# A hybrid decoder layer on one core: block tiles for h, its sums on two engines, and another order of the block products

## The chip, the core and the metric

The kernel runs on one core of a Trainium2 chip. The core has TensorE (PE: matmuls into PSUM), VectorE (DVE), ScalarE (ACT) and GpSimd (POOL) for element-wise work, and SyncE (SP), which here issues every DMA from one queue. Each engine runs its own instructions in order and waits for semaphores of the others. The metric is the time of one execution in microseconds; the kernel before was run three times, and one further execution was profiled. All data are float32. A matmul operand is split into two parts of the type fp32r, hi = round(x) and lo = x - hi, and a product is three matmuls: hi·hi, hi·lo and lo·hi.

## The reference, cut to what matters

```python
h    = rms_norm(x, g_pre)                       # (1024, 1024)
proj = h @ w_in                                 # q,k,v,z_a | u,v_s,z_s | z_m,xBC,dt | 3 x 1024 gate logits
y_att = sliding_window_attention(q, k, v, sinks, rel_bias) * silu(z_a)
y_sg  = u * (tril(w_s) @ LN(v_s) + b_s) * silu(z_s)     # by chunk of 128 rows and group of 128 channels
y_ssm = ssd_mixer(z_m, xBC, dt, ...)            # conv, chunked scan, gated group norm
merged = sum over i of sigmoid(gate_i) * (y_i @ w_br_i)
out    = x + rms_norm(merged @ w_out, g_post)
```

## The kernel before

The sequence has 1024 rows and the model 1024 channels. `hT` holds h transposed, channels on the partitions, as one tile of hi and one of lo parts, each 128 x 8 x 1024; every projection reads it. The work goes through these stages:

1. h is made and transposed (`norm`, `flip`), and the first columns are projected.
2. For each of four groups of the state-space mixer: convolution units, then a scan over eight chunks (`Mix`). `local` makes, for a chunk, the product of B and C and a transposed copy of B in one PSUM tile (pool `ps_tr`, two tiles); DVE masks the product into `gtm` (L549), and ACT copies B into `btok` (L551). `sums` needs a tile of the same pool (L602). Between the scan's small products a stream of projection units (`st`) is run by `st.fill`.
3. Attention, with q, z_a and v_s units in the same stream. A v_s unit takes two weight tiles; `load_w` loads a weight, ACT casts whi (L87) and DVE makes wlo (L88). For each 128 rows the result is copied by ACT (L636) and its row statistics are made by DVE (L637, `bst`), both from PSUM.
4. The sums of h. The u, z_s and half of the gate columns are projected by a scheme of seven products in place of eight for a 2 x 2 split of h (rows by channels) and of w. It needs four sums of the blocks of h: s1, s2, s3, s4. For each of four slices kt POOL adds hi and lo of the four blocks (r, L839), and forms the sums (L842 to L845); ACT and DVE split them into hi and lo (L828, L829). s3 overwrites block (1, 0) of h, once the last v_s product has read it. Beside it run the last v_s tiles.
5. The pair stage. `PairStream` runs units of seven products, 12 matmuls each. A unit loads two weight tiles (`raw`), POOL forms four sums of them (`ts`, L207), ACT and DVE split each operand four products ahead (L224, L225). Every product goes into the pool `ps_mm`, three tiles. What follows a product is in the code: s1, u2, u3, s5 are temporaries in a ring of six (`tp`), and four blocks of the result leave as z (blocks 11 and 21) and u (12 and 22). Eight `zu` units come first, with their silu, the mixing product `sg_mix` and its loads `sg_load` between products by an estimate of their time; six `gate_pair` units follow, whose blocks go through a tanh to DRAM.
6. The branch products. `load_y` fetches one of 32 tiles y from DRAM into `yraw` (two buffers), scales the first 16 by `rsb` on POOL (L962), and splits them on ACT and DVE (L964, L965; y4 and y5 of the first eight on POOL). Twelve slots hold them; three (NPY) can be filled before the space of h is given back. `br_unit` is a projection of eight y's; the first unit takes its operands in the pieces 3, 1, 1, 1, 1, 1. After four units of a set the y's of the next set are loaded, and then the stream is emptied.
7. The output product, its norm and the sum with x.

TensorE's order is that of the code. The order on the other engines is set by a scheduler when the program is built; each keeps to it when it runs.

## Time and profile before

| | |
|---|---|
| runs, median (lowest to highest) | 1917.54 us (1916.57 to 1923.05) |
| profiled execution | 1924.31 us |
| its span | 1922.6 us, mean granted TensorE clock 0.977 of full speed |
| busy, share of the span | PE 95%, DVE 57%, ACT 38%, POOL 30% |

The profile records one execution. A row of a wait names the instruction that waited, the one that released it, and the idle time. A row of a stretch gives the busy time of each engine in it and the TensorE clock that was granted, 1.00 being 2.4 GHz and 0.50 being 1.2 GHz. An engine's idle time costs something only where TensorE waits for it in the end.

### The profile page before, as it was taken

The page shows a single profiled execution, that of the slowest core. Times are in us where ns is not written, and L with a number is a line of the kernel's source. Part 1 is how long each engine was busy: PE and PEld are TensorE (multiplying, and loading weights), DVE is VectorE, ACT ScalarE, POOL GpSimd, SP SyncE. Part 2 cuts the span into 40 slices and gives each one's busy share as a digit, 9 for nine tenths or more (in the row PEclk, how much of TensorE's full clock was granted, in tenths as well). Part 3 has the DMA queues.
Part 4 walks back from the last instruction along what each step waited for, and adds up shares of the span by engine and source line. Part 5 has one row for each costly group of instructions (what it writes and reads, how often), then busy time and mean ns, then how long its engine had stood idle before and what let it go on. Part 6 is the DMA issues. An engine that isn't in the chain of part 4 may idle for free. (4 is left out here: it accounts for less than half of the span.)

```text
span 1922.6 us, 24786 instructions
## 1 busy us (share of the span) xinstructions
PE 1827.9 (95%) x9481; PEld 1540.4 (80%) x9481; DVE 1101.1 (57%) x1546; ACT 724.5 (38%) x1551; POOL 570.9 (30%) x570
## 2 busy tenths in 40 slices
PE   6999999999999999999999779999996999999998
PEld 6888788778877877888888777777885878888898
DVE  5446656675665657466666348887743343535424
ACT  5244454355345434455555222222432120202221
POOL 1001420240132024156666766555724110000000
PEclk9999999999999999999999989999997999999999
DMA  6211431342234134211111122333435453533213
GB/s 218 72 58 55 121 126 44 99 141 62 64 118 121 44 107 127 102 44 56 44 56 56 64 72 73 117 103 116 148 115 203 143 166 97 175 109 111 88 34 143
DMA packets 100663, 192.86 MB, mean 100 GB/s; under 512 B 9376, under 2 KB 55744, under 8 KB 100416
## 3 DMA queue, kind: packets, MB, share of 16 engines
q1 hardware_dynamic: 100544, 191.28, 30.8%
q8 instruction: 74, 1.21, 0.3%
q14 instruction: 45, 0.37, 0.1%
HBM read 152.83 MB, written 38.42 MB: 99 GB/s over the span
## 5 line engine op out<-in xcount | busy, mean ns | idle before, releaser
L105 PE MATMUL ps_mm<-hT,whi 128*128 128x512 f32 x1104 | 436.6, 395 | 0.8 <-DVE z L317 0.8
L107 PE MATMUL ps_mm<-hT,wlo 128*128 128x512 f32 x1104 | 430.2, 390 | 0.0
L106 PE MATMUL ps_mm<-hT,whi 128*128 128x512 f32 x1104 | 430.1, 390 | 0.0
L87 ACT CAST whi<-raw 128x1024 fp32r<-128x1024 f32 (+1 forms) x119 | 124.1, 1043 | 338.1 <-PE ps_mm L106 317.0
L105 PEld LDWEIGHTS ps_mm<-hT,whi 128*128 128x128 f32 x1104 | 207.4, 188 | 44.3 <-issue 2.5
L107 PEld LDWEIGHTS ps_mm<-hT,wlo 128*128 128x128 f32 x1104 | 207.3, 188 | 44.0
L106 PEld LDWEIGHTS ps_mm<-hT,whi 128*128 128x128 f32 x1104 | 207.7, 188 | 40.9
L88 DVE TENSOR_TENSOR wlo<-raw,whi 128x1024 fp32r<-128x1024 f32 (+1 forms) x117 | 152.2, 1302 | 117.7 <-ACT whi L87 117.6
L105 PE MATMUL ps_mm<-y,whi 128*128 128x512 f32 x512 | 202.8, 396 | 12.3 <-ACT y L964 12.3
L106 PE MATMUL ps_mm<-y,whi 128*128 128x512 f32 x512 | 203.2, 397 | 7.1 <-DVE y L965 3.8
L107 PE MATMUL ps_mm<-y,wlo 128*128 128x512 f32 x512 | 202.3, 395 | 0.0
L558 POOL TENSOR_TENSOR y<-xg,dsk 128x512 f32<-128x512 f32 x32 | 39.5, 1245 | 389.8 <-issue 225.5
L499 DVE SCALAR_TENSOR_TENSOR acc<-xr,wcv,acc 128x512 f32<-128x512 f32 x144 | 111.4, 773 | 40.5 <-ACT acc L497 37.1
L105 PEld LDWEIGHTS ps_mm<-y,whi 128*128 128x128 f32 x512 | 98.0, 191 | 34.5 <-ACT y L964 14.1
L106 PEld LDWEIGHTS ps_mm<-y,whi 128*128 128x128 f32 x512 | 97.9, 191 | 30.4 <-DVE y L965 5.7
L107 PEld LDWEIGHTS ps_mm<-y,wlo 128*128 128x128 f32 x512 | 98.0, 191 | 20.4
L78 POOL TENSOR_TENSOR rso<-rso,mhalf_row 128x1 f32<-128x1 f32 x8 | 4.4, 552 | 353.6 <-DVE rso L77 353.6
L996 DVE SCALAR_TENSOR_TENSOR tm<-gld,ps_mm 128x512 f32<-128x512 f32 x48 | 33.0, 687 | 131.5 <-PE ps_mm L107 131.4
L130 PE MATMUL ps_mm<-whi,hT 128*128 128x256 f32 (+1 forms) x256 | 83.0, 324 | 25.7 <-DVE bst L637 11.8
L247 PE MATMUL ps_mm<-hT,whi 128*128 128x512 f32 x224 | 89.8, 401 | 10.3 <-DVE us L259 6.0
L534 ACT ACTIVATE seg<-seg,acs 128x128 f32<-128x128 f32 x256 | 80.9, 392 | 28.2 <-DMA seg<-acs_dr 28.1
L249 PE MATMUL ps_mm<-hT,wlo 128*128 128x512 f32 x224 | 88.6, 396 | 0.0
(223 smaller groups left out, 3728.6 us busy)
## 6 DMA issues: line engine op xcount, KB each, us to landing
seg<-acs_dr SPq DMA_DIRECT2D x32, 512.0 KB, 4.7
yraw<-y_dr SPq DMA_DIRECT2D x32, 512.0 KB, 4.5
raw<-in_w_br_dram SPq DMA_DIRECT2D x32, 512.0 KB, 4.2
gld<-gate_dr SPq DMA_DIRECT2D x32, 512.0 KB, 3.4
raw<-in_w_xbc_dram SPq DMA_DIRECT2D x24, 512.0 KB, 3.6
raw<-in_w_zm_dram SPq DMA_DIRECT2D x16, 512.0 KB, 3.5
y_dr<-y SPq DMA_DIRECT2D x32, 256.0 KB, 2.2
raw<-in_w_zu_dram SPq DMA_DIRECT2D x16, 512.0 KB, 3.7
```

The costliest lines, as they stand in the source:

```text
L87: A.copy(hi, raw)
L88: eng.tensor_tensor(lo, raw, hi.bitcast(F32), op=ALU.subtract)
L105: T.matmul(ps, lhsT=whi[:, ks], rhs=rhs(0, kt, half), start=kt == 0, stop=False)
L106: T.matmul(ps, lhsT=whi[:, ks], rhs=rhs(1, kt, half), start=False, stop=False)
L107: T.matmul(ps, lhsT=wlo[:, ks], rhs=rhs(0, kt, half), start=False, stop=kt == KT - 1)
L130: T.matmul(o, lhsT=lhs(0, kt, tt), rhs=whi[:, ks], start=kt == 0, stop=False)
L247: T.matmul(o, lhsT=hi[:, ks], rhs=h0, start=kt == 0, stop=False)
L249: T.matmul(o, lhsT=lo[:, ks], rhs=h0, start=False, stop=kt == 3)
L499: V.scalar_tensor_tensor(acc, xr[:, k + f0:k + f0 + 512], wcv[:, ti, k:k + 1], acc, op0=ALU.mult, op1=ALU.add)
L534: A.activation(seg[:, j, :], seg[:, j, :], AF.Relu, scale=-1.0, bias=acs[:, c, g * 8 + j:g * 8 + j + 1])
L558: G.tensor_tensor(d["y"], xg[g][:, :, cs], col(dsk, g), op=ALU.mult)
L996: V.scalar_tensor_tensor(tm, gt[0][:, fs], 1.0, ps, op0=ALU.add, op1=ALU.mult)
```

## The change

Five things are changed.

- h is held in eight tiles, `hB[row block, channel block][part]`, each 128 x 4 x 512, instead of two; every reader addresses the same data.
- In the sums of h, the r's move from POOL to DVE, with one buffer each instead of two, and the splits of a slice are written after the stream's next fill, with two buffers for x1, x2 and x4.
- The seven products of a pair unit come in the order B11, T2, T1, T3, B22, T4, B21. Products 2 and 5 use the pool `ps_ac`. u4 has a buffer of its own, where before u2 was overwritten. The blocks are finished in the order 22, 12, 21, 11, and the factor u is applied right behind each silu. Gate pairs stand between zu pairs by ORDER, with `sg_mix` after four products of the next unit; one gate pair is left for the end.
- Two y's (NPY) are loaded before the last gate pair, and `yraw` has four buffers, which also serve the last loads of x. The first branch weight is loaded within the last gate pair. All low parts are made on DVE. The y slots are placed in the freed space ahead of `merged`. The next set of units is added before the stream is empty. The first unit's pieces are 2, 2, 1, 1, 1, 1.
- B is copied by DVE.

The diff, cut to its core:

```diff
-NPY = 3
+NPY = 2
+ORDER = "zgzgzgzgzzzzg"
...
-            src = b[("B11", "T2", "B21", "T3", "T1", "T4", "B22")[i]]
+            src = b[("B11", "T2", "T1", "T3", "B22", "T4", "B21")[i]]
...
-            o = psum(ps_mm, "mm")
+            o = psum(ps_ac, "ac") if i in (2, 5) else psum(ps_mm, "mm")
...
             elif i == 2:
-                block(11, V, t["s1"], o)
+                A.copy(tmp("s5"), o)
+                G.tensor_tensor(tmp("u4"), t["u2"], t["s5"], op=ALU.add)
             elif i == 3:
                 V.tensor_tensor(tmp("u3"), t["u2"], o, op=ALU.add)
+                block(22, G, t["u3"], t["s5"])
             elif i == 4:
-                A.copy(tmp("s5"), o)
-                block(22, G, t["u3"], t["s5"])
-                G.tensor_tensor(t["u2"], t["u2"], t["s5"], op=ALU.add)
+                block(12, V, t["u4"], o)
             elif i == 5:
                 block(21, V, t["u3"], o, ALU.subtract)
             else:
-                block(12, V, t["u2"], o)
+                block(11, V, t["s1"], o)
...
-    hT = [hp.tile([P, KT, S], F32R, name=f"hT{i}") for i in range(2)]
+    hB = {(i, j): [hp.tile([P, 4, 512], F32R, name=f"h{i}{j}{part}") for part in range(2)]
+          for i in range(2) for j in range(2)}
...
-                A.copy(d["b"], pg[:, P:2 * P])
+                V.tensor_copy(d["b"], pg[:, P:2 * P])
...
-                    r[i, j] = bp.tile([P, 512], F32, name=f"r{i}{j}", bufs=2)
-                    G.tensor_tensor(r[i, j], blk(0, i, j)[:, kt, :].bitcast(F32),
-                                    blk(1, i, j)[:, kt, :].bitcast(F32), op=ALU.add)
+                for ij, h in hB.items():
+                    r[ij] = bp.tile([P, 512], F32, name="r%d%d" % ij)
+                    V.tensor_tensor(r[ij], h[0][:, kt, :].bitcast(F32), h[1][:, kt, :].bitcast(F32), op=ALU.add)
...
-            for i, x in ((1, s1), (2, s2), (4, s4)):
-                split(sums[i][0][:, kt, :], sums[i][1][:, kt, :], x)
             st.fill(10.4)
+            if kt > 0:
+                x1, x2, _, x4 = made[kt - 1]
+                for to, x in ((s1, x1), (s2, x2), (s4, x4)):
+                    split(to, kt - 1, x)
...
+        g, late = 0, []
+        for kind in ORDER:
+            if kind == "z":
+                sg_load(g)
+            pst.run(4)
+            for x in late:
+                sg_mix(x)
+            late = []
+            pst.run(3)
+            if kind == "z":
+                late.append(g)
+                g += 1
+    pst.add(*[gate_pair(n) for n in gates_left])
...
-        raw = py.tile([P, S], F32, name="yraw", bufs=2)
+        raw = py.tile([P, S], F32, name="yraw", bufs=4)
...
-        return ct_unit(t["w_br"][un * 8 + dd], rhs, evac, (3, 4, 5, 6, 7, KT) if un == dd == 0 else (KT,))
+        return ct_unit(t["w_br"][un * 8 + dd], rhs, evac, (2, 4, 5, 6, 7, KT) if un == dd == 0 else (KT,))
+    for n in range(NPY):
+        ys[n] = load_y(n)
+    pst.run(3)
+    st.add(*br[:8])
+    st.loaded = st._load()
+    pst.run(4)
+    es7.close()
+    ph1.close()
...
     for un in range(4):
-        st.add(*[br_unit(un, dd) for dd in range(8)])
         st.fill(5.2 * 8)
         if un < 3:
             for n in range(un * 8 + 8, un * 8 + 16):
                 ys[n] = load_y(n)
-        st.drain()
+            st.add(*br[un * 8 + 8:un * 8 + 16])
+            st.fill(5.2 * 8)
+    st.drain()
```

Three places show what the scheduler makes of it. The first is the sums of h, on POOL. A number behind a name tells one buffer's use from another's. Before, the first slice and half of the second read:

```order
L839 TENSOR_TENSOR r00_9646<-hT0_95,hT1_96 128x512
L839 TENSOR_TENSOR r01_9648<-hT0_95,hT1_96 128x512
L839 TENSOR_TENSOR r10_9650<-hT0_95,hT1_96 128x512
L839 TENSOR_TENSOR r11_9652<-hT0_95,hT1_96 128x512
L844 TENSOR_TENSOR s30_9642<-r00_9646,r10_9650 128x512
L842 TENSOR_TENSOR s1_9654<-r10_9650,r11_9652 128x512
L839 TENSOR_TENSOR r00_9783<-hT0_95,hT1_96 128x512
L843 TENSOR_TENSOR s2_9655<-s1_9654,r00_9646 128x512
L839 TENSOR_TENSOR r01_9785<-hT0_95,hT1_96 128x512
L845 TENSOR_TENSOR s4_9656<-r01_9648,s2_9655 128x512
L839 TENSOR_TENSOR r10_9787<-hT0_95,hT1_96 128x512
L839 TENSOR_TENSOR r11_9789<-hT0_95,hT1_96 128x512
```

After the change the first eight POOL sums of the stretch read:

```order
L831 TENSOR_TENSOR x3_9659<-r00_9648,r10_9652 128x512
L829 TENSOR_TENSOR x1_9656<-r10_9652,r11_9654 128x512
L830 TENSOR_TENSOR x2_9657<-x1_9656,r00_9648 128x512
L832 TENSOR_TENSOR x4_9658<-r01_9650,x2_9657 128x512
L831 TENSOR_TENSOR x3_9791<-r00_9780,r10_9784 128x512
L829 TENSOR_TENSOR x1_9788<-r10_9784,r11_9786 128x512
L830 TENSOR_TENSOR x2_9789<-x1_9788,r00_9780 128x512
L832 TENSOR_TENSOR x4_9790<-r01_9782,x2_9789 128x512
```

The sixteen rows L839 have left POOL, and each of its rows is now a sum of two r's or of a sum and an r. In the same place ACT casts the second slice's sums and the last v_s weight; `vst` is a v_s tile's copy. Before:

```order
L828 CAST S10_9633<-s1_9791 128x512
L636 COPY vst_9779<-ps_mm_9754 128x256
L828 CAST S20_9635<-s2_9792 128x512
L87 CAST whi_9506<-raw_9504 128x1024
L828 CAST S40_9637<-s4_9793 128x512
```

After:

```order
L816 CAST S10_9641<-x1_9788 128x512
L816 CAST S20_9639<-x2_9789 128x512
L816 CAST S40_9643<-x4_9790 128x512
L88 CAST whi_9512<-raw_9510 128x1024
L226 CAST whi_10156<-raw_10152 128x512
```

The weight's cast has moved behind the third cast of the slice, so it stands behind POOL's eighth sum, where it stood behind POOL's sixteenth instruction.

The second place is DVE in the pair stage, at the end of a zu unit: the evacuations of products 5 and 6, with `ps_mm` and `ps_ac` the pool that each frees. Before:

```order
L259 TENSOR_TENSOR zs<-tp,ps_mm 128x512
L225 TENSOR_TENSOR wlo<-ts,whi 128x512 x2
L884 SCALAR_TENSOR_TENSOR zs<-th,zs 128x512
L887 SCALAR_TENSOR_TENSOR zs<-us,zs 128x512
L259 TENSOR_TENSOR us<-tp,ps_mm 128x512
L887 SCALAR_TENSOR_TENSOR zs<-us,zs 128x512
```

After:

```order
L261 TENSOR_TENSOR zs<-tp,ps_ac 128x512
L227 TENSOR_TENSOR wlo<-ts,whi 128x512
L227 TENSOR_TENSOR wlo<-raw,whi 128x512
L874 SCALAR_TENSOR_TENSOR zs<-th,zs 128x512
L875 SCALAR_TENSOR_TENSOR zs<-us,zs 128x512
L261 TENSOR_TENSOR zs<-tp,ps_mm 128x512
L874 SCALAR_TENSOR_TENSOR zs<-th,zs 128x512
L875 SCALAR_TENSOR_TENSOR zs<-us,zs 128x512
```

Product 5's evacuation frees a tile of `ps_ac`; two splits, the silu and the factor u still stand between it and product 6's evacuation.

The third place is SP's queue at the end of the pair stage, where `tp` is a gate block, `raw` a branch weight, `gld` a gate tile for a branch unit and `xt` a tile of x for the end. Before, from the last gate blocks on:

```order
L928 DMA gate_dr<-tp 128x512 x3
L84 DMA raw<-in_w_br_dram 128x1024
L989 DMA gld<-gate_dr 128x1024 x2
L957 DMA yraw<-y_dr 128x1024 x2
L1035 DMA xt_15498<-in_x_dram 128x1024
L1035 DMA xt_15534<-in_x_dram 128x1024
L1035 DMA xt_15570<-in_x_dram 128x1024
L957 DMA yraw<-y_dr 128x1024 x2
```

After, from the last blocks of the last gate pair but one on, the first `yraw` being y1:

```order
L955 DMA yraw<-y_dr 128x1024
L915 DMA gate_dr<-tp 128x512
L955 DMA yraw<-y_dr 128x1024 x4
L74 DMA rsb<-rs_dr 128x1024
L85 DMA raw<-in_w_br_dram 128x1024 x2
L915 DMA gate_dr<-tp 128x512 x2
L85 DMA raw<-in_w_br_dram 128x1024
L915 DMA gate_dr<-tp 128x512 x2
L85 DMA raw<-in_w_br_dram 128x1024
L978 DMA gld<-gate_dr 128x1024 x2
L955 DMA yraw<-y_dr 128x1024 x4
```

Four y tiles, y2 to y5, have moved ahead of the last gate pair's stores, and the three loads of x have gone from here.

## Rows read from the trace of the kernel before

**Rows 1.** The page's busy times: engine, us, share of the span, instructions.
```profile
PE 1827.9 (95%) x9481; PEld 1540.4 (80%) x9481; DVE 1101.1 (57%) x1546; ACT 724.5 (38%) x1551; POOL 570.9 (30%) x570
```

**Rows 2.** Waits of TensorE: waiting line, releaser, us in total, times, longest.
```profile
PE ps_tr L602 <- ACT btok L551: 13.9, 8, 3.4
PE ps_mm L105 <- ACT y L964: 12.3, 3, 7.2
PE ps_mm L130 <- DVE bst L637: 11.8, 2, 7.4
...
PE ps_mm L130 <- ACT whi L87: 9.8, 1, 9.8
PE ps_mm L247 <- DVE us L259: 6.0, 4, 2.1
...
PE ps_mm L247 <- DVE zs L259: 3.5, 1, 3.5
```

**Rows 3.** Stretches: length, busy us of the engines, TensorE clock, DMA share, GB/s.
```profile
1450.00:1480.00 30.00, 15.33 (x40) 10.35 (x39) 8.18 (x6) 5.23 (x5) 15.10 (x7) 0.66 0.60 217
1540.00:1580.00 40.00, 36.76 (x149) 29.51 (x148) 20.46 (x20) 11.35 (x11) 5.56 (x2) 0.91 0.56 182
1140.00:1450.00 310.00, 299.72 (x1392) 248.46 (x1391) 223.19 (x270) 103.37 (x179) 163.43 (x104) 0.99 0.35 115
1090.00:1140.00 50.00, 26.78 (x167) 25.88 (x166) 20.80 (x22) 10.91 (x21) 40.59 (x28) 0.73 0.14 41
```

**Rows 4.** Source lines of POOL's sums: ns min/median/max, first and last start.
```profile
L839 POOL TENSOR_TENSOR r<-hT,hT x16: 1259/1289/2254, 1080.5 to 1118.5; 128x512 f32<-128x512 f32 x16
...
L842 POOL TENSOR_TENSOR s<-r,r x4: 1257/1278/1294, 1086.8 to 1121.9; 128x512 f32<-128x512 f32 x4
...
L845 POOL TENSOR_TENSOR s<-r,s x4: 1703/1712/1747, 1092.2 to 1127.2; 128x512 f32<-128x512 f32 x4
```

**Rows 5.** Timeline at the last v_s weight: start, us, instruction, idle before, releaser.
```profile
1102.19 0.62 ACT L828 CAST S<-s 128x512 fp32r<-128x512 f32 x1 [2.00 <-POOL s L843]
1102.71 1.04 ACT L87 CAST whi<-raw 128x1024 fp32r<-128x1024 f32 x1
...
1103.81 0.58 PE L130 MATMUL ps_mm<-whi,hT 128*128 128x256 f32 x1 [9.79 <-ACT whi L87]
```

**Rows 6.** Source line of DVE's splits of the sums, columns as rows 4.
```profile
L829 DVE TENSOR_TENSOR S<-s,S x12: 1084/1100/1758, 1088.7 to 1129.6; 128x512 fp32r<-128x512 f32 x12
L829 DVE TENSOR_TENSOR hT<-s,hT x4: 685/685/693, 1144.0 to 1145.8; 128x512 fp32r<-128x512 f32 x4
```

**Rows 7.** Two stretches at full speed, v_s tiles and pair products, columns as rows 3.
```profile
1080.00:1090.00 10.00, 10.00 (x85) 10.00 (x85) 2.14 (x4) 1.64 (x4) 10.00 (x9) 1.00 0.22 85
1430.00:1440.00 10.00, 10.00 (x46) 8.29 (x45) 3.98 (x5) 2.39 (x4) 0.00 (x0) 1.00 0.43 131
```

**Rows 8.** Timeline of DVE in the pair stage, columns as rows 5.
```profile
1302.96 2.88 DVE L225 TENSOR_TENSOR wlo<-ts,whi 128x512 fp32r<-128x512 f32 x2
...
1307.65 1.57 DVE L887 SCALAR_TENSOR_TENSOR zs<-us,zs 128x512 f32<-128x512 f32 x1
1309.14 0.68 DVE L259 TENSOR_TENSOR us<-tp,ps_mm 128x512 f32<-128x512 f32 x1
```

**Rows 9.** Timeline of one late y slot on POOL, ACT and DVE.
```profile
1468.70 2.34 POOL L962 TENSOR_TENSOR yraw<-yraw,rsb 128x1024 f32<-128x1024 f32 x1 [5.31 <-DMA yraw<-y_dr]
...
1471.08 1.04 ACT L964 CAST y<-yraw 128x1024 fp32r<-128x1024 f32 x1 [8.90 <-POOL yraw L962]
...
1472.15 1.23 DVE L965 TENSOR_TENSOR y<-yraw,y 128x1024 fp32r<-128x1024 f32 x1 [7.68 <-ACT y L964]
```

**Rows 10.** DMA issue of the page: count, KB each, median us to landing.
```profile
yraw<-y_dr SPq DMA_DIRECT2D x32, 512.0 KB, 4.5
```

**Rows 11.** Source line of the B copy, and what it waited for (us, times).
```profile
L551 ACT COPY btok<-ps_tr x32: 242/265/268, 190.0 to 755.0; 128x128 f32<-128x128 f32 x32
...
  DVE gtm L549: 29.6, 20
```

More of the change, by code (lines that the diff above doesn't have):

```diff
@@ L276, in _step, with run @@
             else:
-                block(12, V, t["u2"], o)
+                block(11, V, t["s1"], o)
             return 2.8
-        def fill(self, us):
-            self.debt += us
-            while self.debt > 1.4:
-                c = self._step()
-                if c is None:
-                    self.debt = 0.0
-                    return
-                self.debt -= c
-        def drain(self):
-            while self._step() is not None:
-                pass
-            self.debt = 0.0
+        def run(self, n):
+            for _ in range(n):
+                self._step()
     ph1 = ExitStack()
@@ L812, in hybrid_kernel @@
     es7 = ExitStack()
+    ep = es7.enter_context(tc.tile_pool(name="ep", bufs=1, side="right", reuse_waits="tile"))
+    pst = PairStream(ep, lambda i, part, kt: blocks[i][part][:, kt, :])
     sop = es7.enter_context(tc.tile_pool(name="sop", bufs=1, side="right", reuse_waits="tile"))
-    ep = es7.enter_context(tc.tile_pool(name="ep", bufs=1, side="right", reuse_waits="tile"))
-    sums = {i: [sop.tile([P, 4, 512], F32R, name=f"S{i}{part}") for part in range(2)] for i in (1, 2, 4)}
-    def blk(part, i, j):
-        return hT[part][:, j * 4:(j + 1) * 4, i * 512:(i + 1) * 512]
@@ L821, in h_pair, with split @@
-    def h_pair(i, part, kt):
-        if i in (1, 4, 6):
-            return sums[{1: 2, 4: 1, 6: 4}[i]][part][:, kt, :]
-        return blk(part, *{0: (0, 0), 2: (0, 1), 3: (1, 0), 5: (1, 1)}[i])[:, kt, :]
-    def split(hi, lo, src):
+    s2, s1, s4 = ([sop.tile([P, 4, 512], F32R, name=f"S{i}{part}") for part in range(2)] for i in (2, 1, 4))
+    blocks = [hB[0, 0], s2, s1, hB[1, 0], s4, hB[1, 1], hB[0, 1]]
+    def split(to, kt, src):
+        hi, lo = (x[:, kt, :] for x in to)
         A.copy(hi, src)
@@ L829, in split @@
         V.tensor_tensor(lo, src, hi.bitcast(F32), op=ALU.subtract)
[L831 removed]
     with tc.tile_pool(name="bp", bufs=1, reuse_waits="tile") as bp:
[L833 to L847 removed]
+        made = []
@@ new lines, in hybrid_kernel @@
+        for kt in range(5):
+            if kt < 4:
+                r = {}
+                for ij, h in hB.items():
+                    r[ij] = bp.tile([P, 512], F32, name="r%d%d" % ij)
+                    V.tensor_tensor(r[ij], h[0][:, kt, :].bitcast(F32), h[1][:, kt, :].bitcast(F32), op=ALU.add)
+                x1, x2, x4 = (bp.tile([P, 512], F32, name=f"x{i}", bufs=2) for i in (1, 2, 4))
+                x3 = bp.tile([P, 512], F32, name="x3", bufs=4)
+                G.tensor_tensor(x1, r[1, 0], r[1, 1], op=ALU.add)
+                G.tensor_tensor(x2, x1, r[0, 0], op=ALU.subtract)
+                G.tensor_tensor(x3, r[0, 0], r[1, 0], op=ALU.subtract)
+                G.tensor_tensor(x4, r[0, 1], x2, op=ALU.subtract)
+                made.append((x1, x2, x3, x4))
@@ L848, in hybrid_kernel @@
             st.fill(10.4)
+            if kt > 0:
+                x1, x2, _, x4 = made[kt - 1]
+                for to, x in ((s1, x1), (s2, x2), (s4, x4)):
+                    split(to, kt - 1, x)
         st.drain()
         for kt in range(4):
-            split(blk(0, 1, 0)[:, kt, :], blk(1, 1, 0)[:, kt, :], s3[kt])
+            split(hB[1, 0], kt, made[kt][2])
     with ExitStack() as es:
@@ L929, in gate_pair @@
             return [t["w_gp"][n][k] for k in range(2)], (tile_, evac)
-        pst.add(*[zu_unit(g) for g in range(8)])
         ngp = (24 - NGATE) // 2
-        pst.add(*[gate_pair(n) for n in range(ngp)])
-        for g in range(9):
-            if g < 8:
-                sg_load(g)
-                pst.fill(2.8 * 3)
-            if g > 0:
-                sg_mix(g - 1)
-            if g < 8:
-                pst.fill(2.8 * 4)
+        zu, gates_left = iter(range(8)), iter(range(ngp))
+        for kind in ORDER:
+            if kind == "z":
+                g = next(zu)
+                pst.add(zu_unit(g))
+            else:
+                pst.add(gate_pair(next(gates_left)))
+        g, late = 0, []
+        for kind in ORDER:
+            if kind == "z":
+                sg_load(g)
+            pst.run(4)
[3 more added lines that the diff above has]
+            pst.run(3)
+            if kind == "z":
+                late.append(g)
+                g += 1
+    pst.add(*[gate_pair(n) for n in gates_left])
     py = ctx.enter_context(tc.tile_pool(name="py", bufs=1, reuse_waits="tile"))
@@ L966, in load_y @@
         return hi, lo
-    ys = {}
-    for n in range(NPY):
-        ys[n] = load_y(n)
-    pst.drain()
-    es7.close()
-    ph1.close()
-    pz = ctx.enter_context(tc.tile_pool(name="pz", bufs=1, reuse_waits="tile"))
-    merged = [pz.tile([P, S], F32, name=f"mg{i}") for i in range(8)]
-    for n in range(8, 12):
-        spare[n] = slot(n)
+    ys, pools, merged = {}, [], []
     def br_unit(un, dd):
```

36 lines of the change are left out of this document (14 added, 22 removed).

## Prediction

> **What bounds the kernel now.** I read the engines' shares first, then TensorE's waits, then the stretches in which it lost time, and last the timelines around each loss. TensorE is busy 95% of the span and the next engine 57% [rows 1], so TensorE sets the time and only what makes it stand still, or run at the lower clock, can be won. Its waits [rows 2] are few: 13.9 us in the scan for the B copy, 21.6 us for the last v_s weight and for the row statistics that free its PSUM tiles, 9.5 us in the pair stage for DVE's evacuations, and 12.3 us for the casts of the y operands of the branch products. Each wait costs more than its length, since after it TensorE works for a while at 1.2 instead of 2.4 GHz, so I count a stretch's loss as idle time plus (1 - granted clock) times busy time. From the four stretches [rows 3]: 1090 to 1140 us, where h is summed, 23.2 idle + 0.27 x 26.8 = 30 us; 1140 to 1450, the pair stage, 10.3 + 0.01 x 300 = 13 us; 1450 to 1480, the start of the branch products, 14.7 + 0.34 x 15.3 = 20 us; 1540 to 1580, the change to the second eight y's, 3.2 + 0.09 x 36.8 = 6.5 us. Some 70 us in all, and the change touches every one of the four places, and the B copy as a fifth.
>
> **1. The sums of h.** Before, POOL makes 32 sums without a pause, the first at 1080.5, the last at 1127.2: sixteen r's at 1.29 us and sixteen further sums at 1.28 to 1.71 [rows 4]. ACT's cast whi of the last v_s weight stands behind two casts that need POOL's sixteenth sum: it starts at 1102.71, and TensorE, out of work at 1094.0, waits until 1103.81 [rows 5]. Then the row statistics that free PSUM tiles stand on DVE behind splits that wait for POOL in the same way, 11.8 us [rows 2].
> After: DVE makes the r's. A DVE sum of this shape takes 0.69 us alone and 1.10 beside POOL [rows 6]; POOL keeps sixteen sums. On DVE one statistic more stands before the first r than stood on POOL before 1080.5, so I start at 1082. Three r's, 2.1, bring 1084.0; then whi needs eight POOL sums, half at 1.28 and half at 1.71 [rows 4], 12.0, and I add 1.0 for one r that waits for its single buffer: 1097. The cast that uses the last sum, 0.62, and whi itself, 1.04 [rows 5], bring 1098.7. TensorE waits 4.7 us instead of 9.8, and then 1.6 for wlo as before. The statistics now stand behind DVE work that is already fed: POOL's second eight sums end near 1112, and TensorE takes 2.8 us for a v_s tile (24 matmuls, 85 in 10 us [rows 7]), so I leave 1.5 of the 11.8 us. Idle 23.2 becomes 7.8; the lower-clock part, 7, shrinks in the same ratio to 2. Loss 10 instead of 30: **-20 us**. The sixteen r's, 11 to 18 us of DVE, lie beside v_s products. If every DVE sum also made POOL wait, whi would come near 1102 and each of two statistics waits would keep 3 us: gain 8. If nothing is left but wlo: gain 27.
> Rows 6 and 4 show DVE's split and POOL's sums slowing each other by 0.4 us. The Trainium skill (SBUF — State Buffer, section "Who interferes with whom") says that a DVE instruction with two SBUF inputs and a POOL instruction that reads SBUF exclude each other for their whole length. By that rule eight r's and eight sums run strictly in turn, 8 x 0.69 + 8 x 1.28 = 15.7 us, whi is ready near 1099.3 and a statistics wait of 2 to 3 us stays: the step would be -16 instead of -20. The splits of 1.10 agree with a partial overlap, not with a full lock.
>
> **2. The pair stage.** Work is the same: 98 products, the same sums, splits and evacuations; one add on POOL makes u4 into a buffer of its own. Two things move. Products 2 and 5 go to the other PSUM pool, so the last product of a unit, whose evacuation comes late, no longer blocks product 2 of the next unit but product 3, one product later (12 matmuls at 46 in 10 us [rows 7], 2.6 us). The waits to be won are of that kind: at 1309.14 DVE evacuates product 6 only after two splits (2.88) and the silu of product 5 (its last step 1.57), all slowed by POOL [rows 8], and TensorE stands 2.15 us. Four such waits sum to 6.0, all under 2.6; the first unit's 3.5 [rows 2] is an evacuation behind vg, which in the new order stands two evacuations deeper, with a tile more in hand. Second, a gate pair, which has no silu, stands between z pairs, so DVE's queue empties. I leave 3 of 13 us: **-10 us**. The other end: a gate pair now holds five temporaries and four results in six buffers, and its stores go through SP's one queue between weight loads; were each of five changes from gate to z to cost 2 us, the step would be 0. The best is -13. Later splits of the third sum cost nothing more: four casts and four splits stood before the first product that needs them, and still do.
>
> **3. The start of the branch products.** Before, the chain is: POOL's product 2.34, ACT's cast 1.04, DVE's low part 1.23 [rows 9], and ahead of them a DMA of 4.5 us [rows 10], with two raw buffers, so y5 to y7 are fetched one after the other once TensorE has nothing else. After, two y's are in place and four raw buffers let y2 to y5 be fetched and scaled beside the last gate pair (the SP rows in the part on the change). At the end of the last product, call it t0, the casts stand behind its tanh: first cast at t0 + 1.4, then one per 1.05; low parts of y2 to y5 at t0 + 3.7, 4.9, 6.2 and 7.4. TensorE spends 2.6 us on y0 and y1 in both halves (12 matmuls) and 1.3 on each further y: it waits about 1.5 us for y2 and y3, and reaches y6 near t0 + 9.2. The raw of y6 goes out when y2's buffer is free, t0 + 3.7; plus 4.5 to 5, 2.35, 1.05, 1.24 it is whole at 13.3, y7 at 15.7. Idle: 1.5 + 3.5 + 1, 6 us; with a quarter to a half of that again at the lower clock, 8 us stay of 20: **-12 us**. If the four early raws came late (the queue holds gate stores in front of them) the step is -5; if y6 hid too, -17. Block tiles matter here: each product's h is free by itself, so the new y tiles need not wait for the very last one.
>
> **4. The later changes of eight.** y12 to y15 reuse slots 0 to 3, read last 4.6 to 2.6 us before the end of the last unit (a half is 24 matmuls, 5.2 us), and four raw buffers have them scaled by then. All casts fit ahead of their use: 1 of 6.5 us stays; with 1 us for the two later changes, **-6 us** (-3 to -8).
>
> **5. The B copy.** 32 copies of 0.265 us leave ACT [rows 11] and go to DVE right behind gtm, which frees the other half of the same PSUM tile. In 20 of the 32 cases the copy itself waited for gtm, 29.6 us in all [rows 11], and among them are TensorE's four long waits, 2.4 to 3.4 us: there gtm is late (it stands behind a reduction that waits for ACT), and they stay. The four short ones, under 1.1 each, came from ACT's queue and go. **-1 us**. Upper end if all 13.9 go with their clock: -18; lower end, 32 x 0.28 on the path: +9.
>
> Sum: -20 - 10 - 12 - 6 - 1 = -49 us. The profiled execution took 1924.3 us for a span of 1922.6; it is 6.8 us slower than the median of the runs, and I take the differences over as they stand: 1917.5 - 49 = **1868 us**, with 1850 to 1890 for this case.
>
> **Rivals.**
> (a) The waits change their place: POOL and DVE slow each other more than rows 6 say, the r's single buffers make DVE and POOL wait in turn, and gate stores delay the raws. For it: DVE's splits of 1.44 each in rows 8. Against it: POOL has half the work in the sums, and the pair stage's total is unchanged. Lower ends: -8, -3, -5, -3 and +3, some -16 to -25: 1897.
> (b) Every touched wait goes: -27, -13, -17, -7, -6 = -70: 1848. Against it stand y6 and y7, whose raws have no free buffer.
> (c) Slower: the B copy on DVE. DVE is in order, and its queue in the scan holds operations that wait for ACT and POOL; if the copy stood behind such a wait, the next scan products would come later in each of 32 chunks, and TensorE would fall to the lower clock each time. It outweighs the rest from 49 / 32 = 1.5 us per chunk; at 2.4, as in the long waits, the sum is +28: 1945. Against it: in DVE's order the copy follows gtm at once, or after one product that waits for DVE only.
> (d) Nothing to be seen: in steps 1 and 3 the waits only take other names (statistics behind r's that wait for POOL, y4 and y5 fetched late) and keep their length; the pair stage and the later changes give their lower ends, 3 each, and the B copy costs 3: -3, 1914. Against it: eight POOL sums before whi where sixteen stood.
>
> **Chances.** Forecast 0.66, (a) 0.16, (b) 0.11, (c) 0.03, (d) 0.04. What a measurement can tell from no change is about 0.3%, 6 us. Of (a) nearly all is still faster. Faster 0.93, within 0.3% 0.04, slower 0.03. The range 1846 to 1900 takes in more than half of (a) and of (b).
>
> **What would show it.** In the new trace TensorE waits under 6 us for whi of the last v_s weight and hardly for the statistics; its waits for DVE in the pair stage sum to under 4; at the first branch unit one wait of 2 to 4 us for the cast of y6 is the longest; none at y12; the B wait is now named DVE and is still 10 to 13 us. I am wrong if the stretch of the h sums still holds over 20 us of loss, if waits of 2 us appear at changes from gate pairs to z pairs, or if the scan is longer by over 5 us.

## The result, and the profile after

| | before | changed |
|---|---|---|
| median of four runs (lowest to highest) | 1918.38 us (1916.57 to 1923.05) | 1874.03 us (1872.69 to 1875.96) |
| ratio, with its 95% interval | | 0.9766 (0.9746 to 0.9786) |
| profiled execution, its span | 1924.31, 1922.6 us | 1872.69, 1871.0 us |

The change wins 44 us where 49 were forecast: 1874 against 1868. Between the two profiled executions the difference is 51.6, since that of before is 5.9 us above its median and that of the changed kernel 1.3 below. The page's busy times and TensorE's waits in the changed kernel (waiting line, releaser, us in total, times, longest):

```profile
PE 1809.9 (97%) x9481; PEld 1529.9 (82%) x9481; DVE 1128.5 (60%) x1596; ACT 715.5 (38%) x1519; POOL 552.6 (30%) x552
...
PE ps_mm L106 <- ACT y L962: 11.1, 2, 6.9
PE ps_tr L596 <- DVE btok L545: 10.9, 4, 3.2
...
PE ps_mm L131 <- ACT whi L88: 7.8, 1, 7.8
...
PE ps_mm L131 <- DVE bst L631: 1.8, 1, 1.8
...
PE ps_mm L249 <- DVE zs L261: 0.4, 1, 0.4
...
PE ps_mm L249 <- DVE tp L272: 0.2, 1, 0.2
```

Against [rows 1, 2]: the statistics fell from 11.8 to 1.8 us, the waits of the pair stage for DVE from 10.3 to 0.6 (L247 before, with 0.8 us for `tp` beside the two of [rows 2]; L249 now), the wait for whi only from 9.8 to 7.8, and the waits for the casts of y hardly, from 12.3 to 11.1. The stretches that answer to [rows 3], here in the order sums, pair stage, start of the branch products, change to the second eight y's (length, busy us of the engines, granted clock, DMA share, GB/s):

```profile
1080.00:1120.00 40.00, 29.93 (x216) 29.23 (x215) 32.52 (x38) 13.07 (x27) 23.56 (x15) 0.83 0.18 57
1120.00:1406.00 286.00, 285.33 (x1336) 238.13 (x1335) 209.94 (x262) 94.34 (x167) 153.95 (x102) 1.00 0.35 114
1406.00:1436.00 30.00, 16.91 (x58) 12.40 (x57) 16.42 (x14) 11.11 (x13) 13.80 (x6) 0.77 0.77 279
1500.00:1540.00 40.00, 40.00 (x178) 33.14 (x177) 22.61 (x25) 12.00 (x12) 0.00 (x0) 1.00 0.61 210
```

By the prediction's count (idle plus 1 minus the clock times busy) the losses are 10.1 + 0.17 x 29.9 = 15 us in the sums (30 before, 10 forecast), 0.7 in the pair stage (13, 3), 13.1 + 0.23 x 16.9 = 17 at the start of the branch products (20, 8), and nothing at the later change (6.5, 1). So two terms came out larger than forecast and two smaller.

A sharper measure is the length of a stage, from the first product of one kind to the first of the next. The rows of the changed kernel's source lines that give four of these starts (ns min/median/max, first and last start):

```profile
L719 PE MATMUL ps_ac<-k,q x128: 220/282/365, 795.8 to 1041.7; 128*128 128x256 f32 x112, 128*128 128x128 f32 x16
...
L249 PE MATMUL ps_mm<-h,whi x168: 389/389/470, 1121.6 to 1405.4; 128*128 128x512 f32 x168
...
L106 PE MATMUL ps_mm<-y,whi x512: 387/389/796, 1406.1 to 1771.0; 128*128 128x512 f32 x171
...
L131 PE MATMUL ps_mm<-whi,y x256: 278/283/384, 1771.7 to 1864.0; 128*128 128x256 f32 x128
```

Read in the same way from every profile (us; "start" is up to the first 128x512 product, "scan" from there to the first attention product, "attention and sums" to the first pair product, and so on):

| kernel | start | scan | attention and sums | pair stage | branch products | output | median of runs |
|---|---|---|---|---|---|---|---|
| before | 67.3 | 736.7 | 341.7 | 299.2 | 378.4 | 99.3 | 1918.4 |
| before, a second profile | 65.8 | 733.9 | 342.0 | 299.6 | 376.8 | 99.3 | 1919.1 (one run) |
| changed | 63.9 | 731.9 | 325.8 | 284.5 | 365.6 | 99.3 | 1874.0 |
| B copied by ACT | 63.2 | 733.6 | 325.8 | 284.5 | 366.7 | 99.3 | 1876.7 |
| r's on POOL | 62.3 | 729.8 | **341.7** | 284.5 | 366.6 | 99.6 | 1889.4 |
| two buffers per r | 68.6 | 729.4 | **323.7** | 284.5 | 366.4 | 99.3 | 1875.3 |
| all products in ps_mm | 67.3 | 728.9 | 325.8 | **293.0** | 361.7 | 99.3 | 1877.4 |
| z pairs first | 63.1 | 734.0 | 325.9 | **287.3** | **359.9** | 99.3 | 1871.1 |
| two raw buffers | 63.1 | 729.0 | 325.8 | 284.5 | **382.4** | 102.4 | 1891.2 |
| early casts | 66.9 | 733.7 | 325.8 | 284.5 | **362.9** | 99.3 | 1867.7 |
| early casts, attention first | 62.7 | 728.7 | 325.9 | 284.5 | **348.1** | 99.4 | 1853.9 |
| v_s first halves | 67.6 | 728.8 | 326.4 | 284.4 | 366.6 | 99.3 | 1874.5 |
| four edits | 67.2 | 731.9 | 327.6 | 284.4 | 348.2 | 99.4 | 1858.2 |
| four edits, z pairs first | 66.8 | 729.2 | 327.1 | 286.5 | 348.2 | 99.3 | 1859.9 |

The 51.6 us are 3.4 in the start, 4.8 in the scan, 15.9 in the sums (20 forecast), 14.7 in the pair stage (10) and 12.8 in the branch products (12 + 6).

### The profile page after: what moved, and what is told of

It is laid out like the page before. It is cut to its first block, busy times and chain, and to the rows that moved or that the text cites. A ratio compares the mean times of both kernels' runs of the same rounds, so it can differ in the third digit from the quotient of the medians.

```text
span 1871.0 us, 24800 instructions
## 1 busy us (share of the span) xinstructions
PE 1809.9 (97%) x9481; PEld 1529.9 (82%) x9481; DVE 1128.5 (60%) x1596; ACT 715.5 (38%) x1519; POOL 552.6 (30%) x552
## 3 DMA queue, kind: packets, MB, share of 16 engines
q8 instruction: 74, 1.21, 0.3%
## 5 line engine op out<-in xcount | busy, mean ns | idle before, releaser
L106 PE MATMUL ps_mm<-h,whi 128*128 128x512 f32 x1104 | 436.3, 395 | 0.1
L108 PE MATMUL ps_mm<-h,wlo 128*128 128x512 f32 x1104 | 430.1, 390 | 0.0
L107 PE MATMUL ps_mm<-h,whi 128*128 128x512 f32 x1104 | 430.0, 389 | 0.0
L108 PEld LDWEIGHTS ps_mm<-h,wlo 128*128 128x128 f32 x1104 | 207.2, 188 | 43.9
L106 PEld LDWEIGHTS ps_mm<-h,whi 128*128 128x128 f32 x1104 | 207.4, 188 | 43.5 <-issue 2.2
L107 PEld LDWEIGHTS ps_mm<-h,whi 128*128 128x128 f32 x1104 | 207.6, 188 | 40.7
L89 DVE TENSOR_TENSOR wlo<-raw,whi 128x1024 fp32r<-128x1024 f32 (+1 forms) x117 | 158.2, 1353 | 117.5 <-ACT whi L88 117.5
L106 PE MATMUL ps_mm<-y,whi 128*128 128x512 f32 x512 | 200.8, 392 | 11.1 <-ACT y L962 11.1
L107 PE MATMUL ps_mm<-y,whi 128*128 128x512 f32 x512 | 200.6, 392 | 2.0 <-DVE y L963 2.0
L131 PE MATMUL ps_mm<-whi,h 128*128 128x256 f32 (+1 forms) x256 | 81.6, 319 | 11.3 <-ACT whi L88 7.8
L735 ACT ACTIVATE p<-s,mx 128x129 f32<-128x129 f32 x128 | 50.0, 392 | 96.3 <-DVE mx L731 96.3
L132 PE MATMUL ps_mm<-whi,h 128*128 128x256 f32 (+1 forms) x256 | 80.2, 313 | 1.8 <-DVE h L373 1.8
```

The source lines that it names most:

```text
L89: eng.tensor_tensor(lo, raw, hi.bitcast(F32), op=ALU.subtract)
L106: T.matmul(ps, lhsT=whi[:, ks], rhs=rhs(0, kt, half), start=kt == 0, stop=False)
L107: T.matmul(ps, lhsT=whi[:, ks], rhs=rhs(1, kt, half), start=False, stop=False)
L108: T.matmul(ps, lhsT=wlo[:, ks], rhs=rhs(0, kt, half), start=False, stop=kt == KT - 1)
L131: T.matmul(o, lhsT=lhs(0, kt, tt), rhs=whi[:, ks], start=kt == 0, stop=False)
L132: T.matmul(o, lhsT=lhs(1, kt, tt), rhs=whi[:, ks], start=False, stop=False)
```

## The experiments

Except the first, each edit is made to the changed kernel. All were timed beside the kernel before, whose medians on those chips were 1917.3 to 1923.6 us.

**The kernel before, profiled again.**

> The kernel before, unchanged, profiled a second time. Theory: its first profile was some 6 us above the median of the runs, and this excess lies where the clock fell to 0.95 between 50 and 100 us and to 0.93 between 200 and 250; a second profile takes 1916 to 1920 us, the first 128x512 projection starts near 64 us instead of 67.3, the scan takes some 612 us instead of 615.4, and the three later stages keep their lengths (95.8, 299.2 and 378.4 us). Rival: nothing is by chance, the change itself won the 3.4 us of the start and the 4.8 of the scan; then the second profile shows 67 and 615 again.

1919.1 us; start 65.8, scan 733.9, the three later stages within 1.6 us of the first profile. (The expectation's scan figures, 612 and 615.4, run from the first product of B and C, here 612.6; those of the table from the first 128x512 product.) 4.3 of the 5.2 us by which this span is shorter lie in the start and the scan, so about half of the 8.2 us that the first pair of profiles shows there is the spread of single executions. What was won in the sums, the pair stage and the branch products is the change's.

**B copied by ACT again.**

```diff
-                V.tensor_copy(d["b"], pg[:, P:2 * P])
+                A.copy(d["b"], pg[:, P:2 * P])
```

> The changed kernel with the copy of B back on ACT. Theory: the copy on DVE is worth 1 to 3 us, so 1875 to 1877 us, the scan 1 to 3 us longer and named ACT in TensorE's waits. Rival: the copy gave all 4.8 us that the scan won between the two profiles: 1878 to 1880. Second rival: DVE pays for it, 1872 or less.

1876.7 us, 2.7 above the changed kernel. TensorE's waits for B are 12.9 us in 8 cases, against 10.9 in 4 with DVE's copy:

```profile
PE ps_tr L596 <- ACT btok L545: 12.9, 8, 3.0
```

The four short ones go, the four long ones stay, as in step 5. The scan takes 733.6 to 736.7 us in the three profiles with ACT's copy (mean 734.7) and 728.7 to 734.0 in the eleven with DVE's (730.5). From this and the medians I put the copy at 2 to 4 us, but that is not clear of the spread: the two ranges touch, two of the three profiles with ACT's copy are of the kernel before, and the ratios to before overlap (0.9758 to 0.9792 with ACT's copy, 0.9746 to 0.9786 without). The shorter waits, 2.0 us, are the surest figure.

**The r's on POOL again.**

```diff
-                    V.tensor_tensor(r[ij], h[0][:, kt, :].bitcast(F32), h[1][:, kt, :].bitcast(F32), op=ALU.add)
+                    G.tensor_tensor(r[ij], h[0][:, kt, :].bitcast(F32), h[1][:, kt, :].bitcast(F32), op=ALU.add)
```

> The changed kernel with the sixteen sums of hi and lo (r) back on POOL, splits and order as changed. Theory: sharing the sums between two engines made the stretch short; with r's on POOL the last v_s weight's whi again waits for some sixteen POOL sums, 8 or more us longer, partly won back because splits stand one slice later: 1879 to 1886 us, the wait for whi 13 to 17 us instead of 7.8. Rival: the later splits and the block tiles did it, not the engine: 1873 to 1877. Rival two: all 15.9 us come back, 1888 to 1890.

1889.4 us; attention and sums take 341.7 us, what they took before, and the waits are back:

```profile
PE ps_mm L131 <- ACT whi L88: 11.0, 1, 11.0
...
PE ps_mm L131 <- DVE bst L631: 9.8, 2, 6.4
```

My theory, that the later splits had won a part, fell; the second rival was right. With the splits and tiles as changed, the whole 15.9 us hang on giving sixteen of the 32 sums to another engine; the later splits and the block tiles, without that, moved nothing here. Whether the r's on DVE would win as much with the splits in their old place was not run.

**Two buffers for each r.**

```diff
-                    r[ij] = bp.tile([P, 512], F32, name="r%d%d" % ij)
+                    r[ij] = bp.tile([P, 512], F32, name="r%d%d" % ij, bufs=2)
```

> The changed kernel with two buffers for each of the four r's instead of one. Theory: POOL's pauses before its sums (0.6, 1.2 and 1.8 us in the trace) come from DVE and POOL having to take turns while both read SBUF, and from DVE's other work, not from the buffers: the time from the first attention product to the first pair product stays at 325 to 326 us and TensorE's wait for whi at 7 to 8. Rival: the single buffers make the two engines wait for each other; then POOL runs through, whi comes 2 to 4 us sooner, and the stretch takes 321 to 323.5.

The stretch is 323.7 us, 2.1 shorter, between what the two theories gave; the wait for whi goes from 7.8 to 7.1. So the single buffers cost 2 us of the stretch, about half of the 4.1 that were short of the forecast.

**All seven products in ps_mm.**

```diff
-            o = psum(ps_ac, "ac") if i in (2, 5) else psum(ps_mm, "mm")
+            o = psum(ps_mm, "mm")
```

> The changed kernel with all seven products of a pair in the three tiles of ps_mm again, instead of the third and the sixth in ps_ac. Theory: the tile that a late evacuation holds is met one product sooner, and waits of the kind of 0.5 to 2 us come back at some units: the pair stage takes 287 to 293 us instead of 284.5, 1876 to 1883 us. Rival: the new order of products and of pairs empties DVE's queue so far that three tiles are enough: 284 to 286, 1873 to 1876.

The pair stage takes 293.0 us, 8.5 longer, the upper end of what the theory gave, and waits of the old kind are back, among them:

```profile
PE ps_mm L249 <- DVE tp L272: 2.8, 1, 2.8
...
PE ps_mm L249 <- DVE tp L267: 2.2, 1, 2.2
```

The branch products get 3.9 us of it back (361.7 for 365.6), so that the two stages together lose 4.6.

**All z pairs ahead of the gate pairs.**

```diff
-ORDER = "zgzgzgzgzzzzg"
+ORDER = "zzzzzzzzggggg"
```

> The changed kernel with all eight z pairs in a row and the gate pairs behind them (the order of the kernel before). Theory: a gate pair between z pairs lets DVE's queue empty, and that is a part of the 14.7 us that the pair stage won: the stage takes 287 to 291 us instead of 284.5, with waits of 0.5 to 2 us for DVE at products whose evacuation is late; 1876 to 1881 us. Rival one: the order of pairs did it all, 295 us and more, 1885. Rival two: it did nothing, 284 to 286, 1873 to 1876.

The pair stage takes 287.3 us, 2.8 longer, as the theory gave. But the branch products take 359.9, 5.7 shorter, which no theory had foreseen: over the two stages the mixed order of the changed kernel is 2.9 us worse. The whole times, 1871.1 and 1874.0, agree, but their ratios to before overlap (0.9737 to 0.9766 and 0.9746 to 0.9786).

**Two raw buffers.**

```diff
-        raw = py.tile([P, S], F32, name="yraw", bufs=4)
+        raw = py.tile([P, S], F32, name="yraw", bufs=2)
...
-            xt = py.tile([P, D], F32, name="xt2", tag="yraw", bufs=4)
+            xt = py.tile([P, D], F32, name="xt2", tag="yraw", bufs=2)
```

> The changed kernel with two raw buffers for y instead of four. Theory: the four buffers hide the fetch of y2 to y5 and of y12 to y15; with two the start of the branch products waits 5 to 10 us more and the change at y12 some 4 us, so the branch stage takes 374 to 382 us instead of 365.6 and the time is 1883 to 1890 us. Rival: at the start the casts stand behind the tanhs anyway, so that the four buffers gain nothing there, and only the 3 to 6 us at y12 come back: 369 to 372, 1877 to 1880.

The theory was right, and its upper ends were just passed: the branch products take 382.4 us, 16.8 longer, the whole 1891.2, and the output takes 3.1 longer; the last loads of x share the two buffers, which is the likely cause. TensorE waits 21.7 us for y's in twelve places instead of 13.1 in four, and two stretches answer to [rows 3] nearly line by line:

```profile
1402.00:1432.00 30.00, 15.28 (x40) 10.05 (x38) 10.97 (x9) 8.64 (x11) 10.74 (x5) 0.72 0.55 193
1500.00:1540.00 40.00, 36.48 (x152) 29.20 (x151) 20.47 (x20) 11.35 (x11) 5.45 (x2) 0.96 0.54 177
```

At the change of eight 5 us come back (3.5 idle, 0.04 x 36.5 in clock), and 2.0 of idle time at the two later changes; that leaves some 10 of the 16.8 us for the start, of which the first 30 us show only 2 (19 for 17). Four raw buffers are what hides the fetch at both places.

**Early casts.** The sums S get a stack of their own, which ends after the last unit's fifth product; a pool in its place takes y2 to y5.

```diff
-        return [(py if k < NPY else pz).tile([P, S], F32R, name=f"y{i}", tag=f"y{i}_{k}") for i in range(2)]
+        return [(py if k < NPY else pq if k < 6 else pz).tile([P, S], F32R, name=f"y{i}", tag=f"y{i}_{k}") for i in range(2)]
...
-    pst.run(4)
+    pst.run(2)
+    es_s.close()
+    pq = ctx.enter_context(tc.tile_pool(name="pq", bufs=1, reuse_waits="tile"))
+    for n in range(NPY, 6):
+        ys[n] = load_y(n)
+    pst.run(2)
     es7.close()
```

> The changed kernel, with y2 to y5 put in a pool of their own that takes the place of the sums S as soon as the last unit's fifth product has read them, so that their casts stand on ACT ahead of the last tanhs of the gates. Theory: the wait of 6.9 us for the cast of y2 is the queue behind four tanhs, which wait for DVE's evacuations; it falls to 0 to 2 us and the time to 1863 to 1869, with y6's wait of 4.2 still there or 1 us longer. Rival: POOL's scaling and DVE's low parts set it (all engines are full at that place): the wait only moves to y3 or y4 and the time stays at 1871 to 1876.

1867.7 us, as the theory gave, but the branch products of the profiled execution (1874.8, the slowest of four) are only 2.7 us shorter than the changed kernel's, and this is the surer figure; start and scan spread by several us. The wait for the cast of y2 falls from 6.9 to 0.8 us, and DVE's low part of the same y2 is late in its place, by 5.2 (the next expectation calls it y3; it is the first y behind the products of y0 and y1). So the rival was right in that a wait remains. The wait at y6 is 1.9 instead of 4.2. The timeline (start, us, instruction, idle before, releaser):

```profile
1413.50 5.64 POOL L961 TENSOR_TENSOR yraw<-yraw,rsb 128x1024 f32<-128x1024 f32 x2 [1.50 <-issue]
...
1413.63 3.31 DVE L89 TENSOR_TENSOR wlo<-raw,whi 128x1024 fp32r<-128x1024 f32 x1 [2.18 <-ACT whi L88]
...
1416.87 3.35 DVE L964 TENSOR_TENSOR y<-yraw,y 128x1024 fp32r<-128x1024 f32 x1
...
1420.28 0.80 PE L107 MATMUL ps_mm<-y,whi 128*128 128x512 f32 x1 [5.18 <-DVE y L964]
...
1420.75 1.21 DVE L964 TENSOR_TENSOR y<-yraw,y 128x1024 fp32r<-128x1024 f32 x1
```

Two DVE operations take 3.3 us each while POOL scales two y's, and right after one takes 1.21. The queue of casts behind the tanhs was the first cause; by this timeline POOL's scaling is the second, hidden behind it.

**Early casts, attention's y's first.** On top of the early casts the branch order becomes 2, 0, 1, 3, with gates and weights to match; the attention's y's are not scaled.

```diff
-        gi = (2, 2, 0, 1)[un]
+        gi = (0, 2, 2, 1)[un]
...
-        nc.sync.dma_start(out=raw, in_=y_dr[n])
-        if n < 16:
+        m = (2, 0, 1, 3)[n // 8] * 8 + n % 8
+        nc.sync.dma_start(out=raw, in_=y_dr[m])
+        if m < 16:
```

> The kernel with the early casts of y2 to y5, and the branch products in the order attention, first and second half of the state-space mixer, spatial gating: the first eight y's are then those of the attention, which POOL does not scale. Theory: what is left at the start of the branch products (5.2 us for DVE's low part of y3, 1.9 and 0.8 at y6) comes from POOL's scaling, which DVE has to take turns with (3.35 us for a low part that takes 1.23 alone); without it the branch stage takes 354 to 358 us instead of 362.9, with no wait over 2 us. Rival: the fetches into four raw buffers and ACT's queue set it, the stage stays at 361 to 363.

1853.9 us, ratio to before 0.9646 (0.9623 to 0.9670): the fastest of all runs. The branch products take 348.1 us, 6 less than my best figure, without a wait; the first 30 us of the stage are full at the full clock:

```profile
1401.00:1431.00 30.00, 30.00 (x134) 24.84 (x133) 21.42 (x18) 11.03 (x12) 15.20 (x6) 1.00 0.85 314
```

Until 1409.7 POOL scales nothing here, and till then the low parts take 1.16 to 1.23 us each. Since this stage is full throughout (348.1 us of 348.1), the others' losses can be read from it: 378.4 - 348.1 = 30.3 us in the kernel before, 17.5 in the changed one. The edit takes the scaling of the first eight y's away whole: the slowing of DVE, POOL's own time in the chain, and the load of the scale row `rsb` that POOL needs first. Which of these was worth what was not run apart.

**First halves of v_s first.** For three row tiles the products with the first weight tile, then those with the second (shown for the unit's plan alone).

```diff
-                plan = [(tt, 0, KT - 1) for tt in range(3)] + [(tt, KT - 1, KT) for tt in range(3)] + plan[3:]
+                plan = [(tt, 0, lead) for tt in range(3)] + [(tt, lead, KT) for tt in range(3)] + plan[3:]
...
-        return tc_unit([t["w_vs"][qd - 1][i] for i in range(2)], h_tc, evac, 256)
+        return tc_unit([t["w_vs"][qd - 1][i] for i in range(2)], h_tc, evac, 256, lead=4)
```

> The changed kernel with another order of the products of the v_s units: for the first three row tiles the products with the first weight tile, and then those with the second. Theory: TensorE stops for whi of the last v_s weight because the very first row tile needs both weight tiles, and the second one gets its buffer only when the unit before has ended; with three first halves, 36 matmuls or 4.3 us, ahead of it the wait falls from 7.8 to 3 to 4.5 us and the stretch from the first attention product to the first pair product from 325.8 to 321 to 323 us. Rival: the work that TensorE then has is only taken from behind the wait, and the statistics that free PSUM tiles stop it by the same time: 325 to 326.

The wait for whi is gone, and the stretch is 326.4 us, no shorter. The statistics on DVE stop TensorE instead:

```profile
PE ps_mm L131 <- DVE bst L631: 8.2, 4, 3.8
```

The rival was right: the statistics stand in DVE's queue, which is busy 27.9 of the 32 us from 1081 to 1113 with r's, splits and statistics, and whi was only the wait that ended last.

**Four edits together** (early casts, attention first, first halves of v_s, two buffers per r), and the same with the z pairs first.

> Early casts, attention's branch first, the first halves of v_s first and two buffers for each r together. Theory: the four act at different places and add up: first attention product to first pair product 319 to 322 us (325.8 in the changed kernel), pair stage 284.5, branch stage 354 to 358 (365.6): 1858 to 1864 us. Rival: the time won in the sums only moves the limit to DVE, 322 to 324, and with POOL's scaling not the cause at the branch products 1866 to 1869.

> The same four edits, and all z pairs ahead of the gate pairs. Theory: the pair stage takes 287.3 instead of 284.5, and the branch stage gains less than the 5.7 us that this order gave the changed kernel, since the casts are early already: 0 to 3 us against the run with the four edits, so equal to it within 3 us. Rival: the gains add up in full, 3 us faster.

1858.2 and 1859.9 us, both behind the 1853.9 with two of the edits. The branch products keep their 348.2; the sums come out at 327.6 and 327.1, worse than with either of their two edits, so the theory of adding up failed there, and its total (1858 to 1864) was met only because the branch products won more than it gave them. With early casts and the attention first, the z pairs first cost 2.1 us in the pair stage and bring nothing back, since the branch products have nothing left to win: equal within 3 us, as the theory gave, and the rival of full addition is out.

## Why the prediction was right, point by point

**Step 1, the sums of h: right, a little too large (-20, measured -15.9).** The prediction started the first r at 1082 of the old profile, which is 1081.9 when the changed kernel's times are moved by the 8.2 us of start and scan; the r's then took longer. The changed kernel's rows for [rows 4 to 6]:

```profile
1073.67 4.67 DVE L826 TENSOR_TENSOR r<-h,h 128x512 f32<-128x512 f32 x4
...
1075.45 1.74 POOL L209 TENSOR_TENSOR ts<-raw 128x512 f32<-128x512 f32 x1
...
L826 DVE TENSOR_TENSOR r<-h,h x16: 674/694/1781, 1073.7 to 1103.7; 128x512 f32<-128x512 f32 x16
...
L831 POOL TENSOR_TENSOR x<-r,r x4: 1291/1483/2189, 1077.8 to 1103.5; 128x512 f32<-128x512 f32 x4
L830 POOL TENSOR_TENSOR x<-x,r x4: 1594/1620/1800, 1080.8 to 1107.2; 128x512 f32<-128x512 f32 x4
...
L817 DVE TENSOR_TENSOR S<-x,S x12: 669/1416/1780, 1086.8 to 1111.9; 128x512 fp32r<-128x512 f32 x12
...
1092.51 1.04 ACT L88 CAST whi<-raw 128x1024 fp32r<-128x1024 f32 x1
...
1093.61 0.58 PE L131 MATMUL ps_mm<-whi,h 128*128 128x256 f32 x1 [7.77 <-ACT whi L88]
```

POOL's first sum starts at 1077.8, 1086.0 in the old frame (8.2 us later) and 2.0 us after my 1084.0. The prediction had left out that POOL still makes sums of a pair unit's weights (`ts`) until 1077.2; beside them the first four r's take 4.67 us, 1.17 each instead of 0.69. The eight sums take 14.1 instead of 13, the single buffers being 2 us of the stretch. So whi is 3.0 us late, and TensorE waits 7.8 instead of 4.7 us. The place, the queue and the sign were right, and that all of it hangs on the engine of the r's is shown by putting them back. (In the old kernel only the second of the two casts before whi, at 1102.19, needs POOL's sixteenth sum; the forecast does not change by it.)

The lower figure of 16 us, which I gave beside the sum for the rule of the Trainium skill ("SBUF — State Buffer", section "Who interferes with whom"), met the measured 15.9. That alone would be chance, 2.1 us of the gap being buffers. But the early-casts timeline bears the rule out: POOL's two scalings (2.34 each, [rows 9]) and DVE's two low parts (1.2 each) are 7.1 us one after the other and 4.7 side by side, and from 1413.50 to 1420.22 the four take 6.7, nearly strictly in turn. The Trainium skill adds, in the same section, that a DVE instruction with at most one SBUF input, outside the 2-port modes, does not contend with GpSimd. That agrees: in the changed kernel two evacuations from PSUM (1412.04 and 1412.64 in the timeline of step 3) take their usual 0.68 beside the same scaling.

The prediction read the splits of 1.10 us in [rows 6] as "a partial overlap, not a full lock". The kernel before shows otherwise, at 128x512 too:

```profile
1088.00 1.29 POOL L839 TENSOR_TENSOR r<-hT,hT 128x512 f32<-128x512 f32 x1
...
1088.72 1.12 DVE L829 TENSOR_TENSOR S<-s,S 128x512 fp32r<-128x512 f32 x1 [3.86 <-ACT S L828]
1089.25 1.74 POOL L843 TENSOR_TENSOR s<-s,r 128x512 f32<-128x512 f32 x1
```

This split starts 0.57 us before POOL's r ends, and ends 0.55 behind it; POOL's next sum takes 0.45 longer than the one ahead of it. A split that starts late in a POOL sum has only the rest of it to wait out, so a mean of 1.10 says nothing against turns. An r that starts with a whole POOL sum ahead of it takes up to 1.78 (row L826 above), about its own 0.69 and most of POOL's 1.29. A mean over operations that start at different points of the other engine's operation hides this; single rows of the timeline show it.

**Step 2, the pair stage: right, too small (-10, measured -14.7, the best end having been -13).** I had counted 13 us of loss and left 3. The clock behind the 13 is read to two places, and half a hundredth of 300 us is 1.5; the stage had 14 to 15 to lose, and all went. Taken out alone, products 2 and 5 in the other pool cost 8.5 us and the gate pairs between 2.8; edits undone one at a time need not add up, and the remaining 3.4 was not run by itself. It may belong to the order of the products, to u4's own buffer, or to two of these together. The feared waits at changes from gate to z did not come.

**Step 3, the start of the branch products: the step that failed (-12, measured -5).** The failed sentence, which put one tanh ahead of the casts, is "the casts stand behind its tanh: first cast at t0 + 1.4". t0 is 1406.1 here, and the casts of y2 to y5 begin at 1414.81, t0 + 8.7:

```profile
1390.79 11.15 POOL L960 TENSOR_TENSOR yraw<-yraw,rsb 128x1024 f32<-128x1024 f32 x4 [6.66 <-DMA rsb<-rs_dr]
...
1403.47 0.38 SPq L74 DMA_DIRECT2D rsb<-rs_dr  x1
...
1407.26 0.63 ACT L913 ACTIVATE tp<-tp 128x512 f32<-128x512 f32 x1 [8.95 <-POOL tp L261]
...
1408.69 5.64 POOL L960 TENSOR_TENSOR yraw<-yraw,rsb 128x1024 f32<-128x1024 f32 x2 [1.47 <-issue]
...
1408.86 3.26 DVE L89 TENSOR_TENSOR wlo<-raw,whi 128x1024 fp32r<-128x1024 f32 x1 [2.19 <-ACT whi L88]
1412.04 0.68 DVE L261 TENSOR_TENSOR tp<-tp,ps_ac 128x512 f32<-128x512 f32 x1
...
1412.64 0.67 DVE L261 TENSOR_TENSOR tp<-tp,ps_mm 128x512 f32<-128x512 f32 x1
1412.81 0.63 ACT L913 ACTIVATE tp<-tp 128x512 f32<-128x512 f32 x1 [3.45 <-DVE tp L261]
...
1414.81 3.87 ACT L962 CAST y<-yraw 128x1024 fp32r<-128x1024 f32 x4
...
1415.90 0.80 PE L106 MATMUL ps_mm<-y,whi 128*128 128x512 f32 x1 [6.89 <-ACT y L962]
...
1428.08 0.79 PE L106 MATMUL ps_mm<-y,whi 128*128 128x512 f32 x1 [4.21 <-ACT y L962]
```

Four tanhs, not one, and two casts of branch weights stand ahead of the casts; the third tanh waits for DVE's evacuation, which stands behind the low part of a branch weight, 3.26 us beside POOL's scaling. The raws were not what was late: the last of them, y5's, landed 0.6 us after t0. (The prediction's own -5 stood for late raws; that the measured -5 equals it is chance.) The chain also lacked a term. "Fetched and scaled beside the last gate pair" held for y2 and y3 alone, which POOL scales with y0 and y1 from 1390.79. For y4 and y5 it needs the next scale row `rsb`, which has one buffer: its load is issued at 1403.47 and lands at 1408.57, and the two are scaled from 1408.69 to 1414.33, t0 + 2.6 to t0 + 8.2, side by side with that low part. That y6 would wait, 2 to 4 us by the forecast, came true (4.2). The stage's loss was 30.3 us, some 22 of it up to 1500 us; 17.5 stay, all at the start. The two runs with early casts show what the causes are worth: the casts' place in ACT's queue, 2.7 us; this and the scaling of the first eight y's, all 17.5. How much of the scaling's part is the late `rsb`, and what the block tiles, the early branch weight and the new pieces did here, was not run apart.

**Step 4, the later changes: right (-6, measured -8, the rest of the 12.8).** No wait is left there. **Step 5, the B copy: right in its mechanism (-1; 2.0 in TensorE's waits, 2 to 4 by scans and medians, which is not clear of their spread).** The long waits stay, now named DVE; the short ones go.

Steps 1 and 3 had promised 11 us too much, steps 2, 4 and 5 some 8 too little; the total came out as near as it did by these errors cancelling, which is luck. Rivals (b), (c) and (d) did not occur. Of rival (a) its mechanism, POOL and DVE slowing each other, did, in steps 1 and 3; its size did not in step 1, and in step 3 not by the late raws that it named.

## What to carry to other kernels

When raw data come early, walk the queue of every engine between the data and the product, and count what stands ahead there and whom that waits for; here four tanhs and a late scale row held up data that had been fetched in time. An order that keeps TensorE full in one stage can hand its backlog to the next, so judge it by two stages together, and by stage lengths: over kernels with the same code there, those of the sums and the pair stage repeat to 0.4 us and that of the branch products to 1.6, where the whole time varies by several. Choosing first the work that needs fewest engines (y's without a scaling) won more at this seam, 14.8 us, than the reordering of the casts on which it stood, 2.7.

## What the runs showed of the hardware

DVE and POOL took turns, nearly strictly, in operations that both read two tiles in SBUF: at 128x1024 a DVE operation of 1.23 us took 3.3 beside POOL, at 128x512 one of 0.69 took up to 1.78, and one that read PSUM and one SBUF tile kept its 0.68. The first stage, up to the first 128x512 product, took from 62.3 to 68.6 us over the fourteen profiles though its code is the same in all but two; what decides it stays open.
